# Seven-product block form for three gate pairs and half of the values, and 512-wide values for the rest

## The chip, the cores and the metric

The kernel runs on one core of one Trainium2 chip. The metric is the device time of one execution in microseconds (us). The engines are TensorE (PE in the profile; PEld is its loading of weights), VectorE (DVE), ScalarE (ACT), GpSimd (POOL) and SyncE (SP), which issues most transfers.

## The reference

A trunk of two layers over 512 frames of width 1024. Layer 0 is a gated linear recurrence with 8 heads of 128, layer 1 attends over a shared K and V; each is followed by an MLP (1024 to 4096 and back) with squared ReLU, and every part is normed before and after. The change touches the recurrence's projections alone:

```python
proj = h @ w_in                                   # h: rms_norm(x), 512 x 1024; w_in: 1024 x 4096
q, f, i, g = split(proj, 4)                       # each 512 x 1024, 8 heads of 128 columns
q = silu(q); log_f, k = from f
S_t = diag(f_t) S_(t-1) + k_t v_t^T;  o_t = S_t^T q_t      # v = i, chunk by chunk
o = rms_norm(o, gate_norm_w) * silu(g)
out = o @ w_out
```

## The kernel before

Everything is float32. A product in full precision is made of three matmuls (`mm3`): both operands are split into a high part and a remainder (`whi`, `wlo` for weights, `xhi`, `xlo` for the normed input, `uhi`, `ulo` for what the next projection reads), and high x high, high x remainder and remainder x high are added up in PSUM. x is kept transposed, 128 rows by 8 blocks `kt` by 512 frames. The scale 1/rms of each frame is applied after the projections: `rb` along a row, `rcol` as a column.

Weights come in pieces of 512 KB. `fetch_w` loads a piece into one of four `raw` slots through SyncE's queue; a split writes it into one of eight `whi` and one of eight `wlo` slots. `split_w` does it by a ScalarE copy (high part) and a VectorE subtraction (remainder). `load_d` does it by two ScalarE copies (minus the high part into `wlo`, then the high part) and a transfer issued by POOL that adds the same weights from memory onto `wlo`. A slot is free again when the last matmul that reads it is done.

The order of TensorE's instructions is written out by hand. A `Plan` keeps a clock `t` that each matmul advances by a planned duration; `main` yields work, chains that are spawned (one per head, `head`) come in when their planned time is there, and `until(...)` holds back whoever yields it until keys are `done`. The constants `W_...` are the planned waits. What chains issue on the other engines is put ahead of other work there.

In the recurrence (`hgrn`) `main` goes through four pairs p of heads: the projections `qf` of q and f of both heads (`wmm`, weights stationary, 512 frames moving), then the pair's values `i` (`xmm`, x stationary, 256 columns moving, so that frames become rows), then its gates `g` (weights stationary, 512 wide). A head's chain is: gating of q and f by `gate`; then seven levels of doubling length (`gl`), each some matmuls, two VectorE products and a masked copy (first `g0` with `qc`, at the end a transposition `kt`, and `rec` is done); then, once the pair's gates are there, the state `st`, the output `o`, `head_norm` (`hn_a`) and `store_u` into `uhi`, `ulo`, after which `mix` is done. The head after next starts its levels when `mix` is done. The series of products `tt` of each head runs on POOL.

```python
            if p >= 1:
                yield until(("rec", 2 * p - 1))
            if p >= 2:
                yield until(("mix", 2 * p - 4), ("mix", 2 * p - 3))
            wv = (load_w(w_i[p], 256, None, f"wi{p}") if p == 0 else load_d(w_i[p], 256, f"wi{p}"))
```

After the last gates comes the out-projection `ao_h` (`by_halves`): for the first 256 frames it goes over `kt`, 24 matmuls of 256 columns each, and waits for `mix` of head 6 before step 6 and of head 7 before step 7.

At the start `first_loads` brings in x and the first weights, and `start` makes the sum of squares (`squares`), `rcol`, and from it through `dg` and the matmul `ps_sp` the row `rb`, for which the first two heads wait. PSUM has four banks of tag `mm` (`mmt`) and four of tag `sm` (`smt`). The MLP's up-projection already uses a seven-product block form (class `Pair`, tiles `ux`, `uy`, `uz`): a 2 x 2 block product by seven products of blocks (256 frames by half of the columns by half of the rows) and sums of blocks.

## Time and profile before

| what | value |
| --- | --- |
| median of 3 runs | 1274.45 us (1273.57 to 1278.37) |
| the profiled execution | 1276.38 us, its span 1274.6 us |
| PE busy | 1252.4 us, 98% |
| DVE busy | 786.4 us, 62% |
| ACT busy | 660.9 us, 52% |
| POOL busy | 94.0 us, 7% |
| moved by DMA | 160.37 MB, mean 126 GB/s |

The recurrence takes the first 260 us or so of the span. In a group's row the columns are line, engine, operation, output and inputs, shape and count, then busy time, mean duration in ns of one and the idle time before them with what ended it. A row of waits names who waited for whom, the total, the times and the longest. A row of the chain or of a timeline begins with its start and length in us. In the rows by stretch each engine's busy time stands with its number of instructions, then PE's granted clock, the share of DMA time and GB/s. Durations of matmuls in groups include their pipeline; the rate is read from the chain, as length over count.

### The profile page before, as it was taken

To read this page: it belongs to the slowest core of one execution; us is meant where nothing else is said; L and a number is where in the kernel's file an instruction comes from. 1 tells how busy PE (TensorE), PEld (TensorE's weight loads), DVE (VectorE), ACT (ScalarE), POOL (GpSimd) and SP (SyncE) were. 2 spreads that over 40 slices of the span, in tenths; PEclk is the share of its full clock that TensorE was granted. 3 is DMA by queue.
4 is the path that set the end of the run, shared out by engine and by line. 5 is a ranking of instruction groups with operands and counts; after the bars stand their busy time and mean duration, and the time that the engine had idled before them with its cause. 6 is when DMAs were issued, how large, how long until landed. Compare 5 with 4: busy or idle time off the path is not lost.

```text
span 1274.6 us, 21364 instructions
## 1 busy us (share of the span) xinstructions
PE 1252.4 (98%) x8452; PEld 1135.6 (89%) x8452; DVE 786.4 (62%) x1590; ACT 660.9 (52%) x1222; POOL 94.0 (7%) x169
## 2 busy tenths in 40 slices
PE   9999999999999999999999999999999999999996
PEld 7889898999988989989999788889998998988996
DVE  6866556747954635637388977663875463654645
ACT  6553635237832724616356876663773461561732
POOL 0221212010000000000100000001000000000000
PEclk9999999999999999999999999999999999999998
DMA  7655654224366564635525322232425454463522
GB/s 241 165 129 120 148 129 105 67 76 140 113 166 127 164 142 110 182 83 149 182 76 190 115 85 84 83 98 69 166 100 149 100 179 102 116 182 83 160 89 67
DMA packets 56438, 160.37 MB, mean 126 GB/s; under 512 B 6385, under 2 KB 8690, under 8 KB 56338
## 3 DMA queue, kind: packets, MB, share of 16 engines
q1 hardware_dynamic: 45008, 119.82, 30.2%
q0 software_dynamic: 11088, 39.07, 14.8%
q8 instruction: 66, 1.08, 0.3%
q14 instruction: 34, 0.28, 0.1%
q10 hardware_dynamic: 242, 0.13, 0.0%
HBM read 149.29 MB, written 9.70 MB: 125 GB/s over the span
## 4 chain that ended last, share of the span: by engine, by line
PE 83%; DMA 7%; DVE 4%; ACT 4%; issue 2%; SPq 0%; DVEq 0%; ACTq 0%; POOLq 0%
PE dn L114 20%; PE up L114 7%; PE dn_h L114 7%; PE ux L114 6%; PE kq L114 6%; PE qf L114 5%; PE g L114 4%; DMA raw_s<-in_w_us_dram 4%; PE i L114 3%; PE bo_h L114 3%; PE ao_h L114 3%; PE uz L114 3%; PE gl L114 3%; PE v L114 3%; PE lg L114 2%
## 5 line engine op out<-in xcount | busy, mean ns | idle before, releaser
L114 PE MATMUL dn<-uhi,whi_dn 128*128 128x512 f32 x384 | 151.9, 396 | 0.0
L114 PE MATMUL dn<-uhi,wlo_dn 128*128 128x512 f32 x384 | 151.9, 396 | 0.0
L114 PE MATMUL dn<-ulo,whi_dn 128*128 128x512 f32 x384 | 151.8, 395 | 0.0
L114 PEld LDWEIGHTS dn<-uhi,whi_dn 128*128 128x128 f32 x384 | 72.1, 188 | 17.8 <-ACT r L555 0.7
L482 ACT ACTIVATE whi_a<-raw_a 128x1024 fp32r<-128x1024 f32 x24 | 25.4, 1060 | 120.3 <-PE dn L114 116.6
L114 PEld LDWEIGHTS dn<-uhi,wlo_dn 128*128 128x128 f32 x384 | 72.1, 188 | 17.5
L114 PEld LDWEIGHTS dn<-ulo,whi_dn 128*128 128x128 f32 x384 | 72.1, 188 | 16.9
L170 DVE TENSOR_TENSOR wlo_dn<-raw_dn,whi_dn 128x1024 fp32r<-128x1024 f32 x64 | 76.6, 1220 | 6.3 <-ACT whi_dn L169 4.6
L447 DVE TENSOR_TENSOR ulo<-r,uhi 128x1024 fp32r<-128x1024 f32 (+1 forms) x40 | 40.2, 1010 | 56.7 <-ACT uhi L446 56.7
L114 PE MATMUL up<-xhi,whi_up 128*128 128x256 f32 x256 | 72.7, 284 | 0.0
L114 PE MATMUL up<-xhi,wlo_up 128*128 128x256 f32 x256 | 72.0, 281 | 0.0
L114 PE MATMUL up<-xlo,whi_up 128*128 128x256 f32 x256 | 71.9, 281 | 0.0
L169 ACT ACTIVATE whi_dn<-raw_dn 128x1024 fp32r<-128x1024 f32 x64 | 65.8, 1052 | 7.5 <-PE up L114 3.0
L114 PE MATMUL dn_h<-uhi,whi_dn 128*128 128x256 f32 x240 | 67.8, 282 | 0.0
L114 PE MATMUL dn_h<-ulo,whi_dn 128*128 128x256 f32 x240 | 67.4, 281 | 0.0
L114 PE MATMUL dn_h<-uhi,wlo_dn 128*128 128x256 f32 x240 | 67.4, 281 | 0.0
L602 DVE TENSOR_TENSOR zacc<-dn,zacc 128x512 f32<-128x512 f32 x32 | 22.1, 691 | 59.1 <-PE dn L114 59.0
L504 POOL DMA_DIRECT2D raw_s<-in_w_us_dram x24 | 20.8, 866 | 493.8 <-DMA raw_s<-in_w_us_dram 268.0
L114 PE MATMUL qf<-xhi,whi_qf 128*128 128x512 f32 x128 | 52.9, 413 | 0.8 <-ACT xhi L673 0.6
L482 ACT ACTIVATE whi_t<-raw_a 128x1024 fp32r<-128x1024 f32 x24 | 25.5, 1061 | 49.4 <-PE dn L114 27.2
L114 PE MATMUL qf<-xlo,whi_qf 128*128 128x512 f32 x128 | 50.7, 396 | 0.3 <-DVE xlo L674 0.3
L114 PE MATMUL qf<-xhi,wlo_qf 128*128 128x512 f32 x128 | 50.6, 396 | 0.0
(387 smaller groups left out, 4082.2 us busy)
## 6 DMA issues: line engine op xcount, KB each, us to landing
raw_dn<-in_w_dn_dram SPq DMA_DIRECT2D x64, 512.0 KB, 4.6
raw_a<-in_w_us_dram SPq DMA_DIRECT2D x24, 512.0 KB, 4.4
raw_s<-in_w_us_dram SPq DMA_DIRECT2D x48, 256.0 KB, 4.2
raw_s<-in_w_us_dram POOLq DMA_DIRECT2D x24, 512.0 KB, 6.4
raw_up<-in_w_up_dram SPq DMA_DIRECT2D x16, 512.0 KB, 3.7
raw_wkv<-in_w_kv_dram SPq DMA_DIRECT2D x16, 512.0 KB, 3.8
raw_qf<-in_w_qf_dram SPq DMA_DIRECT2D x14, 512.0 KB, 5.8
raw_d<-in_w_us_dram SPq DMA_DIRECT2D x12, 512.0 KB, 4.2
```

The costliest lines, as they stand in the source:

```text
L114: nc.tensor.matmul(out, lhsT, rhs, **kw)
L169: last_split[:] = [a.activation(hi, raw, AF.Copy)]
L170: v.tensor_tensor(lo, raw, hi.bitcast(F32), op=ALU.subtract)
L447: v.tensor_tensor(ulo[pr][:, :, lo:hi], r, uhi[pr][:, :, lo:hi].bitcast(F32), op=ALU.subtract)
L482: a.activation(hi, raw, AF.Copy)
L504: g.dma_start(rs, ws[p, :, 0:2, :], accum_op=ALU.add)
L602: v.tensor_tensor(z, pss[n4], z, op=ALU.add)
```

## The change

The gates of pairs 1 to 3 (`gates_pair`) and the values of pairs 2 and 3 together (`values_pairs`) are computed by seven block products each, 256 wide, over four blocks of weights and sums of them; the weights lie in memory as four blocks (`w_gs`, `w_is`). Of the sums, those with three or more terms are made by VectorE, and the first ones by a transfer issued by POOL that adds one block onto another in `raw`. Blocks as they are go through `split_d` (as in `load_d`), sums through `split_b` (ScalarE copy, VectorE subtraction). The four sums of x's blocks, with the gains applied, are made once by `block_sums`, a chain that is spawned when the first values are done; they use two `raw` slots while they are made, and three of them stay in `whi` and `wlo` slots, the fourth in `uhi[3]`, `ulo[3]`. x itself stays in the memory of `uhi` (`xraw`) for that, so `squares` no longer overwrites it. The values of pairs 0 and 1 are computed together in pair 0, 512 columns wide. `main` no longer waits for `rec` and `mix` ahead of the values but for `po` (the outputs `o` are issued) and `mix` ahead of the values and gates. `ea`, a row used from the out-projection on, shares the memory of `rb`.

```diff
+    xraw = [cp.tile([P, 2, S], F32, tag=f"uhi{i}", name=f"xraw{i}", bufs=1) for i in range(4)]
+    uhi = [cp.tile([P, 2, S], F32R, tag=f"uhi{i}", name=f"uhi{i}", bufs=1) for i in range(4)]
...
+    nrcol = cp.tile([P, 4], F32, name="nrcol")
+    ea = rb
...
+    def split_d(raw, src, name):
+        n, ncols = raw.shape[1:]
+        hi = wp.tile([P, n, ncols], F32R, tag="whi", name=f"whi_{name}", bufs=8)
+        lo = wp.tile([P, n, ncols], F32R, tag="wlo", name=f"wlo_{name}", bufs=8)
+        a.activation(lo, raw, AF.Copy, scale=-1.0)
+        a.activation(hi, raw, AF.Copy)
+        g.dma_start(lo, src.bitcast(F32R), accum_op=ALU.add)
+        return [(hi[:, j, :], lo[:, j, :]) for j in range(n)]
+    def split_b(raw, name):
+        n, ncols = raw.shape[1:]
+        hi = wp.tile([P, n, ncols], F32R, tag="whi", name=f"whi_{name}", bufs=8)
+        lo = wp.tile([P, n, ncols], F32R, tag="wlo", name=f"wlo_{name}", bufs=8)
+        a.activation(hi, raw, AF.Copy)
+        v.tensor_tensor(lo, raw, hi.bitcast(F32), op=ALU.subtract)
+        return [(hi[:, i, :], lo[:, i, :]) for i in range(n)]
...
-        xs = [hp.tile([P, S], F32, tag="g", name=f"raw_x{kt}", bufs=4) for kt in range(2)]
-        x2 = [wp.tile([P, 2, S], F32, tag="raw", name="raw_x2", bufs=4)]
-        x2 += [hp.tile([P, 2, S], F32, tag="sc", name=f"raw_x{2 * pr}", bufs=2) for pr in (2, 3)]
-        xs += [t[:, j, :] for t in x2 for j in range(2)]
+        xs = [xraw[kt // 2][:, kt % 2, :] for kt in range(8)]
...
-        sq = [hp.tile([P, 2, S], F32, tag="vt", name=f"sqx{pr}", bufs=2) for pr in range(2)]
+        sq = [hp.tile([P, 2, S], F32, tag="vt", name=f"sqx{pr}", bufs=3) for pr in range(4)]
         with tc.issue_after(last_split[0].ins):
-            for kt in range(4):
-                a.activation(sq[kt // 2][:, kt % 2], xs[kt], AF.Square)
-            for kt in range(4, 8):
-                a.activation(xs[kt], xs[kt], AF.Square)
-        v.tensor_tensor(sq[0], sq[0], sq[1], op=ALU.add)
-        for i in range(2):
-            v.tensor_tensor(xs[4 + i], xs[4 + i], xs[6 + i], op=ALU.add)
-            v.tensor_tensor(sq[0][:, i], sq[0][:, i], xs[4 + i], op=ALU.add)
+            for pr in range(4):
+                a.activation(sq[pr], xraw[pr], AF.Square)
+        for pr in range(1, 4):
+            v.tensor_tensor(sq[0], sq[0], sq[pr], op=ALU.add)
...
+    def block_sums(xs, ts):
+        gain = gn[:, G_APRE:G_APRE + 8]
+        e, f = [wp.tile([P, 4, 256], F32, tag="raw", name=f"sum_x{i}", bufs=4) for i in range(2)]
+        def split(src, sign, n):
+            if n < 3:
+                hi, lo = [wp.tile([P, 4, 256], F32R, tag=t, name=f"{t}_x{n}", bufs=8) for t in ("whi", "wlo")]
+            else:
+                hi, lo = [u[3].rearrange("p j (r t) -> p (j r) t", r=2) for u in (uhi, ulo)]
+            a.activation(hi, src, AF.Copy, scale=sign)
+            if sign > 0:
+                v.tensor_tensor(lo, src, hi.bitcast(F32), op=ALU.subtract)
+            else:
+                v.scalar_tensor_tensor(lo, src, -1.0, hi.bitcast(F32), op0=ALU.mult, op1=ALU.subtract)
+            ts.append([(hi[:, r, :], lo[:, r, :]) for r in range(4)])
+        def odd(n, out, op):
+            for r in range(4):
+                v.scalar_tensor_tensor(out[:, r], xs[2 * r + 1][:, n * 256:n * 256 + 256], gain[:, 2 * r + 1:2 * r + 2],
+                                       out[:, r], op0=ALU.mult, op1=op)
+        for r in range(4):
+            for n, t in enumerate((e, f)):
+                a.activation(t[:, r], xs[2 * r][:, n * 256:n * 256 + 256], AF.Copy, scale=gain[:, 2 * r:2 * r + 1])
+        v.tensor_tensor(e, e, f, op=ALU.subtract)
+        split(e, 1.0, 0)
+        yield 8.0
+        odd(1, f, ALU.subtract)
+        split(f, 1.0, 1)
+        yield 8.0
+        odd(1, e, ALU.add)
+        split(e, -1.0, 2)
+        yield 8.0
+        odd(0, e, ALU.subtract)
+        split(e, -1.0, 3)
...
+            done(("po", h))
...
+        def banks(name):
+            return [mmt(f"{name}_{n}") for n in "xyz"]
+        def gates_pair(p):
+            src, nm = w_gs[p - 1], f"gs{p}"
+            ra = wp.tile([P, 2, 512], F32, tag="raw", name=f"raw_a{nm}", bufs=4)
+            nc.sync.dma_start(ra, src[:, 0:3:2, :])
+            rs = wp.tile([P, 2, 512], F32, tag="raw", name=f"raw_s{nm}", bufs=4)
+            for i in range(2):
+                nc.sync.dma_start(rs[:, i, :], src[:, 3, :])
+            g.dma_start(rs, src[:, 0:2, :], accum_op=ALU.add)
+            rd = wp.tile([P, 1, 512], F32, tag="raw", name=f"raw_d{nm}", bufs=4)
+            nc.sync.dma_start(rd, src[:, 1:2, :])
+            a11, a12 = split_d(ra, src[:, 0:3:2, :], f"a{nm}")
+            s3, s1 = split_b(rs, f"s{nm}")
+            v.tensor_tensor(ra[:, 0, :], ra[:, 0, :], rs[:, 1, :], op=ALU.add)
+            v.tensor_tensor(ra[:, 1, :], ra[:, 1, :], ra[:, 0, :], op=ALU.add)
+            s2, s4 = split_b(ra, f"t{nm}")
+            a22, = split_d(rd, src[:, 1:2, :], f"d{nm}")
+            x, y, z = [b[:, 0:256] for b in banks(nm)]
+            g0, g1 = ggs[2 * p], ggs[2 * p + 1] = [hp.tile([P, S], F32, tag="g", name=f"g_{2 * p + j}", bufs=4) for j in range(2)]
+            lo, hi = slice(0, 256), slice(256, 512)
+            t1, t3, t2, t4 = ts
+            def prod(ps, w, b, first):
+                for k in range(4):
+                    mm3(ps, w[0][:, k * P:(k + 1) * P], w[1][:, k * P:(k + 1) * P], *b[k], first and k == 0, k == 3, True)
+                    yield 0
+            def swish(gg, sign):
+                if sign > 0:
+                    v.tensor_tensor(gg, gg, rb, op=ALU.mult)
+                else:
+                    v.scalar_tensor_tensor(gg, gg, -1.0, rb, op0=ALU.mult, op1=ALU.mult)
+                e = hp.tile([P, S], F32, tag="e", name=f"e{nm}{sign}", bufs=1)
+                a.activation(e, gg, AF.Sigmoid)
+                v.tensor_tensor(gg, gg, e, op=ALU.mult)
+            yield from prod(x, a11, xpart(0, 0), True)
+            a.activation(g0[:, lo], x, AF.Copy)
+            yield from prod(z, s1, t1, True)
+            a.activation(g1[:, hi], z, AF.Copy)
+            yield from prod(y, a12, xpart(1, 0), True)
+            v.tensor_tensor(g0[:, lo], y, g0[:, lo], op=ALU.add)
+            yield from prod(x, s2, t2, False)
+            a.activation(g0[:, hi], x, AF.Copy)
+            yield from prod(z, s4, xpart(1, 1), False)
+            v.tensor_tensor(g0[:, hi], z, g0[:, hi], op=ALU.add)
+            swish(g0, 1)
+            yield from prod(x, s3, t3, False)
+            v.tensor_tensor(g1[:, hi], x, g1[:, hi], op=ALU.add)
+            a.activation(g1[:, lo], x, AF.Copy)
+            yield from prod(y, a22, t4, True)
+            v.tensor_tensor(g1[:, lo], y, g1[:, lo], op=ALU.add)
+            swish(g1, -1)
+        def values_pairs():
+            nm = "is"
+            def raw(n):
+                return wp.tile([P, 1, 1024], F32, tag="raw", name=f"raw_{n}{nm}", bufs=4)
+            def block(n, i):
+                r = raw(n)
+                nc.sync.dma_start(r, w_is[:, i:i + 1, :])
+                return r
+            def summed(n, i):
+                r = block(n, 3)
+                g.dma_start(r, w_is[:, i:i + 1, :], accum_op=ALU.add)
+                return r
+            ra = block("a", 0)
+            a11, = split_d(ra, w_is[:, 0:1, :], f"a11{nm}")
+            rs = summed("s1", 1)
+            s1, = split_b(rs, f"s1{nm}")
+            rb_ = block("b", 2)
+            a12, = split_d(rb_, w_is[:, 2:3, :], f"a12{nm}")
+            v.tensor_tensor(ra, ra, rs, op=ALU.add)
+            s2, = split_b(ra, f"s2{nm}")
+            v.tensor_tensor(rb_, rb_, ra, op=ALU.add)
+            s4, = split_b(rb_, f"s4{nm}")
+            s3, = split_b(summed("s3", 0), f"s3{nm}")
+            a22, = split_d(block("d", 1), w_is[:, 1:2, :], f"a22{nm}")
+            x, y, z = [b.rearrange("p (m f) -> p m f", m=2) for b in banks(nm)]
+            v0, v1 = vts[2], vts[3] = [hp.tile([P, 4, 256], F32, tag="vt", name=f"vt{p}", bufs=3) for p in (2, 3)]
+            t1, t3, t2, t4 = ts
+            def prod(ps, w, b, first):
+                for m in range(2):
+                    for k in range(4):
+                        f = slice(k * 256, k * 256 + 256)
+                        mm3(ps[:, m, :], *[t[:, m * P:(m + 1) * P] for t in b[k]], w[0][:, f], w[1][:, f],
+                            first and m == 0 and k == 0, k == 3, True)
+                        yield 0
+            def keep(out, ps, n, r):
+                for m in range(2):
+                    tt = 2 * n + m
+                    a.activation(out[:, tt, :], ps[:, m, :], AF.Copy, scale=r[:, tt:tt + 1])
+            def more(out, ps, n, r):
+                for m in range(2):
+                    tt = 2 * n + m
+                    v.scalar_tensor_tensor(out[:, tt, :], ps[:, m, :], r[:, tt:tt + 1], out[:, tt, :], op0=ALU.mult, op1=ALU.add)
+            yield from prod(x, a11, xpart(0, 0), True)
+            keep(v0, x, 0, rcol)
+            yield from prod(z, s1, t1, True)
+            keep(v1, z, 1, nrcol)
+            yield from prod(y, a12, xpart(1, 0), True)
+            more(v0, y, 0, rcol)
+            yield from prod(x, s2, t2, False)
+            keep(v0, x, 1, rcol)
+            yield from prod(z, s4, xpart(1, 1), False)
+            more(v0, z, 1, rcol)
+            yield from prod(x, s3, t3, False)
+            more(v1, x, 1, nrcol)
+            keep(v1, x, 0, nrcol)
+            yield from prod(y, a22, t4, True)
+            more(v1, y, 0, nrcol)
...
-            if p >= 1:
-                yield until(("rec", 2 * p - 1))
-            if p >= 2:
-                yield until(("mix", 2 * p - 4), ("mix", 2 * p - 3))
-            wv = (load_w(w_i[p], 256, None, f"wi{p}") if p == 0 else load_d(w_i[p], 256, f"wi{p}"))
-            vt = vts[p] = hp.tile([P, 4, 256], F32, tag="vt", name=f"vt{p}", bufs=2)
-            for t2 in range(2):
-
-                ps = (smt if p == 0 else mmt)(f"i{p}_{t2}").rearrange("p (j t) -> p j t", j=2)
-                yield from values(ps, wv, t2)
-                if p == 0 and t2 == 0:
-                    yield until("rcol")
-                keep_values(vt, ps, t2)
             if p == 0:
+                wv = load_w(w_i, 512, None, "wi")
+                vts[0], vts[1] = [hp.tile([P, 4, 256], F32, tag="vt", name=f"vt{i}", bufs=3) for i in range(2)]
+                for tt in range(4):
+                    ps = (smt if tt < 2 else mmt)(f"i{tt}")
+                    for kt in range(8):
+                        xmm(ps, wv, kt, 512, tt * P, kt == 0, kt == 7)
+                        yield 0
+                    if tt == 0:
+                        yield until("rcol")
+                    for i in range(2):
+                        a.activation(vts[i][:, tt, :], ps[:, i * 256:(i + 1) * 256], AF.Copy, scale=rcol[:, tt:tt + 1])
                 yield until("rb")
-            wt = load_d(w_g[p], 256, f"wg{p}") if p else load_w(w_g[p], 256, None, f"wg{p}")
-            for j in range(2):
-                ps = mmt(f"g{p}_{j}")
-                for kt in range(8):
-                    wmm(ps, wt, kt, j * P, xhi, xlo, 0, S, kt == 0, kt == 7)
-                    yield 0
-                gg, sg = gate(ps, "g", 2 * p + j)
-                v.tensor_tensor(gg, gg, sg, op=ALU.mult)
-                ggs[2 * p + j] = gg
+                spawn(block_sums(xs, ts), 2.0)
+                wt = load_w(w_g, 256, None, "wg")
+                for j in range(2):
+                    ps = mmt(f"g0_{j}")
+                    for kt in range(8):
+                        wmm(ps, wt, kt, j * P, xhi, xlo, 0, S, kt == 0, kt == 7)
+                        yield 0
+                    gg, sg = gate(ps, "g", j)
+                    v.tensor_tensor(gg, gg, sg, op=ALU.mult)
+                    ggs[j] = gg
+            else:
+                yield until(("po", 2 * p - 2), ("po", 2 * p - 1))
+                if p >= 2:
+                    yield until(("mix", 2 * p - 4), ("mix", 2 * p - 3))
+                if p == 2:
+                    yield from values_pairs()
+                yield from gates_pair(p)
```

The argument lists, the layout of the weights on the host and the moved helper `xpart` are left out here.

More of the change, by code (lines that the diff above doesn't have):

```diff
@@ L186, in load_d, with xpart @@
         for pr in range(ncols // 128):
-            raw = fetch_w(src, ncols, pr, name)
-            hi = wp.tile([P, per, ncols], F32R, tag="whi", name=f"whi_{name}_{pr}", bufs=8)
-            lo = wp.tile([P, per, ncols], F32R, tag="wlo", name=f"wlo_{name}_{pr}", bufs=8)
-            a.activation(lo, raw, AF.Copy, scale=-1.0)
-            a.activation(hi, raw, AF.Copy)
-            g.dma_start(lo, src[:, per * pr:per * (pr + 1), :].bitcast(F32R), accum_op=ALU.add)
-            out += [(hi[:, j, :], lo[:, j, :]) for j in range(per)]
-        return out
+            out += split_d(fetch_w(src, ncols, pr, name), src[:, per * pr:per * (pr + 1), :], f"{name}_{pr}")
+        return out
+    def xpart(j, n):
+        lo, hi = halves[n]
+        return [(xhi[r][:, j, lo:hi], xlo[r][:, j, lo:hi]) for r in range(4)]
     def load_w(src, ncols, gain, name):
@@ L451, in block @@
         b11, b12, b21, b22 = [zb[:, :, j, lo:hi] for j in range(2) for lo, hi in halves]
-        def xpart(j, n):
-            lo, hi = halves[n]
-            return [(xhi[r][:, j, lo:hi], xlo[r][:, j, lo:hi]) for r in range(4)]
         def sums_x():
@@ L475, in sums_x @@
             return parts
-        def split_b(raw, name):
-            n = raw.shape[1]
-            hi = wp.tile([P, 2, 512], F32R, tag="whi", name=f"whi_{name}", bufs=8)[:, 0:n, :]
-            lo = wp.tile([P, 2, 512], F32R, tag="wlo", name=f"wlo_{name}", bufs=8)[:, 0:n, :]
-            a.activation(hi, raw, AF.Copy)
-            v.tensor_tensor(lo, raw, hi.bitcast(F32), op=ALU.subtract)
-            return [(hi[:, i, :], lo[:, i, :]) for i in range(n)]
         a22s = []
@@ L709, in start @@
         rsqrt_col(mean_cols([ssum[:, j, :] for j in range(2)], S, onesd), EPS, rcol)
+        v.tensor_scalar(nrcol, rcol, -1.0, None, op0=ALU.mult)
         done("rcol")
@@ L1064, in main @@
             spawn(start(hp, xs, maskf))
-            yield from hgrn(hp, w0)
+            yield from hgrn(hp, w0, xs)
             proj = out_proj(w_ao, gn[:, G_GATE:G_GATE + 1], "ao",
```

24 lines of the change are left out of this document (13 added, 11 removed).

## The prediction

> **What bounds the kernel now.** I read four views in this order: the head of the page, the engines' waits up to 300 us, the chain that ended last in order of time, and the timelines of single engines where the chain leaves TensorE.
>
> ```profile
> span 1274.6 us, 21364 instructions
> PE 1252.4 (98%) x8452; PEld 1135.6 (89%) x8452; DVE 786.4 (62%) x1590; ACT 660.9 (52%) x1222; POOL 94.0 (7%) x169
> PE ps_sp L114 <- DVE dg L713: 1.2, 1, 1.2
> ...
> 98.00:160.00 62.00, 62.00 (x405) 55.13 (x404) 35.31 (x95) 29.45 (x58) 10.15 (x20) 1.00 0.60 135
> ```
>
> TensorE is busy 98% of the span at full clock. After its 1.2 us wait for `dg` (at about 35 us, the longest that the list has up to 300 us) it does not stop in the recurrence: in 98 to 160 it is busy 62.00 of 62.00 us, with VectorE at 35.31 and ScalarE at 29.45. So what the change takes off TensorE counts in full, and every stall that it makes counts in full too. The chain gives the rates:
>
> ```profile
> 36.82 9.11 PE i L114 x78
> 204.52 11.19 PE qf L114 x48
> 404.60 1.43 PE ux L114 x12
> 406.02 1.44 PE uz L114 x12
> ```
>
> (start, length, instructions.) A 512-wide matmul takes 11.19/48 = 0.2331 us, a 256-wide one of the values 9.11/78 = 0.1168, and one of the seven-product form (already used in the MLP) 1.435/12 = 0.1196. Width costs in proportion, the last form 2.5% more.
>
> **The change part by part.**
>
> Matmuls. A gate pair was 2 x 8 x 3 = 48 at 0.2331 = 11.19 us; it becomes 7 x 4 x 3 = 84 at 0.1196 = 10.05. Three pairs: -3.4 us. Values of the last four heads: 192 become 7 x 2 x 4 x 3 = 168, same form as `i` (x stationary): 24 x 0.1168 = -2.8. Values of the first four: 192 at 0.1168 = 22.43 become 96 of 512 at 0.2331 = 22.38: -0.05. Together **-6.3 us**. The page on matmuls would have it otherwise:
>
> By the Trainium skill ("TensorE: Matmul & The Clock Gate", "Back-to-back issue gap") a sustained stream spaces N=128 at about 81 ns and N=512 at about 131, so a straight line gives about 98 for 256, an estimate. A gate pair would then go from 6.3 to 8.2 us and be a loss, and the term would be +5.8 - 2.3 - 6.2 = -2.7. The rows above (233 ns and 117 to 120) do not agree, and I take the rows.
>
> The start. Here the trace shows how tight the recurrence's first chain is (VectorE's timeline, then ScalarE's, then VectorE by stretches):
>
> ```profile
> 27.45 0.16 DVE L225 TENSOR_SCALAR nx<-ps_mc 128x4 f32<-128x4 f32 x1 [2.30 <-PE ps_mc L114]
> 27.53 1.23 DVE L170 TENSOR_TENSOR wlo_wi<-raw_wi,whi_wi 128x1024 fp32r<-128x1024 f32 x1
> ...
> 33.82 1.23 DVE L170 TENSOR_TENSOR wlo_qf<-raw_qf,whi_qf 128x1024 fp32r<-128x1024 f32 x1 [0.18 <-ACT whi_qf L169]
> 34.96 0.68 DVE L713 TENSOR_TENSOR dg<-ident,rcol 128x512 f32<-128x512 f32 x1
> 47.08 0.43 ACT L772 ACTIVATE qc<-q 128x256 f32<-128x256 f32 x1
> 47.87 2.76 PE L114 MATMUL g<-qc,k 128*128 128x192 f32 x16
> ...
> 20.00:30.00 10.00, 10.00 (x53) 8.42 (x52) 7.36 (x12) 7.08 (x9) 0.00 (x0) 1.00 0.55 188
> 30.00:40.00 10.00, 8.81 (x60) 7.68 (x59) 8.25 (x17) 4.47 (x5) 0.00 (x0) 1.00 0.81 268
> 40.00:50.00 10.00, 10.00 (x74) 9.59 (x74) 8.88 (x16) 9.20 (x16) 6.90 (x16) 1.00 0.43 144
> ```
>
> From 27.45 `rcol`'s eleven small operations run one after the other up to `dg` at 34.96, and five weight splits of about 1.23 us (the first and the last stand here) have slipped in between. TensorE waits for `dg`, and the last `qc` (ready 47.51) is used at 47.87, a margin of 0.4. The change puts two more splits of `w_i` before this, and `block_sums`: on VectorE one subtraction (1.23 by L170's form), twelve of 128x256 (0.42, as L808 below) and four splits (1.23) = 11.2 us; on ScalarE eight scaled copies (0.47, as `vt` below) and four splits of 1.05 (L190's form, below) = 8.0.
>
> ```profile
> L808 DVE TENSOR_TENSOR k<-k,tt 128x256 f32<-128x256 f32 x48 | 20.2, 420 | 0.0
> L911 ACT ACTIVATE vt<-i,rcol 128x256 f32<-128x256 f32 x16 | 6.6, 467 | 16.6 <-PE i L114 16.6
> ```
>
> VectorE has 30 - 7.36 - 8.25 - 8.88 = 5.5 us free between 20 and 50. `block_sums` waits for no data but x, so part of it lands in the gaps of the two chains, and part in 50 to 80, where the levels have room. Least: 0 (all of it later; below nothing is excluded, as it only adds work there). Most: each of the six gaps that are still unfilled takes one more split of 1.05 net, 6.3. The nearest row is the wait of before, 1.2 us with five of eleven gaps filled; with two or so more filled I take **+2.0**. The squares cost the same, since four 128x1024 activations replace eight halves; `nrcol` is one operation of 0.16 beside them.
>
> Evictions. Each product is copied or added out by an operation of 0.42 to 0.47 us; a bank is read again two or three products later (1.43 us each), except `x` between the second block of sums and the next product, with one product between. A split of 1.05 us ahead of it on ScalarE makes 1.05 + 0.47 = 1.52, 0.1 late, three times. The rest of ScalarE's and VectorE's new work per stage (some 4 us each) lies beside TensorE (62.00 against 35.31). `ea` in `rb`'s place and x in `uhi`'s cost nothing: no instruction is added, `uhi`'s next writer is the first head's store behind its whole chain, and `ea` is first written after the out-projection.
>
> Weights' ring. x's sums pin three of the eight `whi`/`wlo` slots until the last gate pair, so five go round. Two of the four raw slots serve the sums at the start only.
>
> ```profile
> L190 ACT ACTIVATE wlo_qf<-raw_qf x8: 1041/1044/1051, 84.1 to 163.1; 128x1024 fp32r<-128x1024 f32 x8
> L192 POOL DMA_DIRECT2D wlo_qf<-in_w_qf_dram x8: 862/870/880, 85.5 to 164.5; - x8
> DMA to landing us min/median/max: 7.4/8.0/9.6
> ...
> 85.48 0.88 POOL L192 DMA_DIRECT2D wlo_qf<-in_w_qf_dram x1 [4.29 <-ACT os_a L626]
> 133.36 2.80 PE qf L114 x12
> ```
>
> From a free slot to a usable block: two copies of 1.05, 0.87 to issue, 8.0 to land = 11.0 us. Before, the block issued at 85.48 is read at 133.36, 40 us after landing. After, a value block lasts 24 x 0.1168 = 2.8 us, four blocks ahead are 11.2, and the heads' own matmuls stretch that. Of 62 us the main stream has 4 x 11.2 = 44.8, so the factor is 62/44.8 = 1.38 and the lead 15.5 us against 11.0. I take **+0.3** with the evictions; ends 0 and, late by 1 us on each of the eleven accumulated blocks of the last two stages, +11. SyncE issues four loads per gate pair instead of two and five for the values instead of four, each waiting for a raw slot as before. POOL issues three accumulating transfers per gate pair instead of two and five for the values instead of four (0.87 each); the new one into `raw_s` waits for the loads under it, and behind it stand the `tt` products of the next head:
>
> ```profile
> 145.97 0.61 POOL L811 TENSOR_TENSOR tt<-ek 128x256 f32<-128x256 f32 x1 [9.64 <-DVE nt L231]
> 158.98 1.30 PE g L114 x8
> ```
>
> They run 13 us before that head's first matmul, so a landing of 8 us in front of them is covered, and I count nothing.
>
> The tail. The last two heads lose 11.2 us of values as cover.
>
> ```profile
> 225.56 0.35 PE i L114 x3
> 231.87 0.65 PE g L114 x4
> ...
> 258.01 0.33 PE kt L119 x3
> 261.88 1.34 PE st L114 x12
> 263.56 3.12 PE o L114 x28
> 279.56 0.44 PE hn_a L119 x4
> 272.05 0.37 ACT L626 ACTIVATE os_a<-o,yh 128x128 f32<-128x128 f32 x1 [0.42 <-DVE os_a L624]
> 281.91 0.69 DVE L636 TENSOR_TENSOR ulo<-g,uhi 128x512 fp32r<-128x512 f32 x1 [0.70 <-ACT uhi L635]
> ```
>
> From the end of the last `qf` (225.56) head 7 needs 6.3 to its first matmul (231.87), 26.5 to the end of its levels (258.34), 3.5 to `st`, 4.8 to the end of `o` (266.68), 5.7 to its normed rows (272.42; the order holds `hn` back until 279.56, but they are ready), 0.44, and 2.6 to `ulo` (282.60): 49.8 us. TensorE has in that time: gates 10.05, out-projection steps 0 to 6, 7 x 24 x 0.1168 = 19.6, and two heads at 8.6 (half of 62 - 44.8 = 17.2) = 46.9. So it idles 49.8 - 46.9 = 2.9 before the last step; before, with 11.2 more values and 1.1 more gates, cover was 59. Ends: 0 (if the levels come nearer to the 23.0 us of head 6) and +8 (if `hn` is held for the planned time). **+2.9.**
>
> Sum: -6.3 + 2.0 + 0.3 + 2.9 = -1.1. The profiled execution took 1276.38 us (span 1274.6), so 1275.3; it lay 1.9 above the median of the three runs, 1274.45, from which -1.1 gives **1273.3**.
>
> **The rivals.** *Nothing is given back*: start and tail hide in what the scheduler finds. For it: TensorE shows no wait from 37 to 290 now, and the order by hand leaves head 7 12.9 us from `o` to `hn` (266.68 to 279.56) where 5.7 suffice. Against: margin 0.4 at `qc`, and 2.9 short at the tail. 1274.45 - 6.3 = 1268.1. *The ring starves* (slower): accumulated blocks come late in the stages with values and last gates. For it: a lead cut from 40 us to 15.5; ScalarE already sits waiting for slots (7.9 us in the row below), with the chain's activations queued behind. Against: 15.5 is over 11.0. It decides when queues on ScalarE and POOL add more than 4.5 us; eleven blocks late by 1 us each: 1273.3 + 11 = 1284.3.
>
> ```profile
> ACT wlo_wi L190 <- PE i L114: 7.9, 3, 7.3
> ```
>
> *Half-width products cost more than half*: the page's rule, as a term of -2.7 instead of -6.3: 1273.3 + 3.6 = 1276.9. The MLP's rows speak against it. That the change does not do what it says I exclude but for the values' first half, which is no saving.
>
> **How the numbers follow.** A measurement of this kernel tells about 0.5% (6.4 us) from no change. Forecast 0.57, nothing given back 0.20, ring 0.20, half-width 0.03. Faster needs under 1268.1: most of the second case, 0.17. Slower needs over 1280.8: most of the ring and a little of the forecast's upper end, 0.23. Else 0.60. The range: below, -6.3 with half a us for what else may shift, 1267.5; above, start 6.3, tail 4 and ring 4 against -6.3 are +8, 1282.5, which leaves out the ring's worse half. The forecast's own range is 1269 to 1278.
>
> **What would show it.** Right: gate products at 1.43 us per 12, 10.0 us per pair; a wait for `dg` of 2 to 4 us near 36; a gap of 1 to 4 us before the out-projection's last step, released by `ulo`; that step's end about 4 us earlier than 287.5. Wrong: TensorE waiting for `whi` or `wlo` in the stages of heads 4 to 7 (ring), waits at `gl` for VectorE (sums in the levels), or no waits at all (then 1268).

## The result, and the profile after

The changed kernel takes 1282.2 us (median of 5 runs, 1281.38 to 1283.12) against 1273.94 us of the kernel before on the same chip: a ratio of 1.0059, interval 1.0041 to 1.0076. The forecast was 1273.3 and "no change"; the time lies in its range, at the upper end, but it moved the other way: 8.3 us slower where 1.1 us faster was forecast. The profiled execution took 1281.38 us.

The head of the page after, TensorE's three longest waits in the recurrence, and its busy time in the stretch up to the first matmul of `up` (busy time with instructions, granted clock, DMA share, GB/s):

```profile
span 1279.3 us, 21468 instructions
PE 1241.0 (97%) x8440; PEld 1125.2 (88%) x8440; DVE 820.6 (64%) x1646; ACT 674.1 (53%) x1248; POOL 100.2 (8%) x171
PE o L114 <- DVE st L879: 11.5, 3, 6.3
PE g L114 <- ACT qc L812: 1.8, 2, 1.3
PE qf L114 <- DMA wlo_qf<-in_w_qf_dram: 1.4, 1, 1.4
0.00:326.50 326.50, 307.55 (x2040) 0.97 0.48 127
```

TensorE is busy 11.4 us less than before (1241.0 against 1252.4) and the span is 4.7 us longer. Up to the first matmul of `up` it is busy hardly less (307.55 us against 307.88), so most of the 11.4 lies behind the recurrence, and in the recurrence waits came. The wait for `dg` is no longer in the list; in its place stands one of 11.5 us, `o` for `st`, in three pieces. Where they lie is read from TensorE's timeline, and what held `st` from VectorE's, POOL's and SyncE's:

```profile
217.69 0.39 PE L114 MATMUL o<-vt,sc 128*128 128x128 f32 x2
224.41 0.80 PE L114 MATMUL o<-st,q 128*128 128x128 f32 x2 [6.33 <-DVE st L879]
...
213.13 0.69 DVE L936 TENSOR_TENSOR g<-g,egs2-1_2039 128x512 f32<-128x512 f32 x1 [0.93 <-ACT egs2-1_2039 L935]
223.41 0.69 DVE L915 TENSOR_TENSOR raw_ags<-raw_ags,raw_sgs 128x512 f32<-128x512 f32 x1 [9.58 <-DMA raw_sgs<-in_w_gs_dram]
224.01 1.12 DVE L879 SCALAR_TENSOR_TENSOR st<-st,tt,st 128x128 f32<-128x128 f32 x4
...
207.12 0.81 SPq L909 DMA_DIRECT2D raw_sgs<-in_w_gs_dram  x2
216.07 0.85 POOL L910 DMA_DIRECT2D raw_sgs<-in_w_gs_dram  x1 [5.02 <-DMA raw_sgs<-in_w_gs_dram]
```

`st` itself is 1.12 us of work and its inputs are there. But in VectorE's queue the addition of L915 stands ahead of it, and that waits for `raw_sgs`: the two loads under it are issued at 207.12, POOL can issue the accumulating transfer at 216.07, and it lands at 223.4. For 9.58 us VectorE does nothing, with `st` of two heads behind the addition, and TensorE stands 6.33 us. At 87 to 92.5 the same picture costs 4.84 us:

```profile
90.33 0.69 DVE L915 TENSOR_TENSOR raw_ags<-raw_ags,raw_sgs 128x512 f32<-128x512 f32 x1 [7.63 <-DMA raw_sgs<-in_w_gs_dram]
92.54 0.80 PE L114 MATMUL o<-st,q 128*128 128x128 f32 x2 [4.84 <-DVE st L879]
```

The waits cost more than their length. Rows by stretch (busy time of PE, PEld, DVE, ACT, POOL, then PE's granted clock):

```profile
92.00:98.00 6.00, 5.46 (x28) 5.14 (x29) 3.19 (x19) 2.28 (x16) 0.00 (x0) 0.72 0.03 6
...
219.00:224.00 5.00, 0.00 (x0) 0.00 (x0) 0.59 (x1) 0.00 (x0) 0.00 (x0) 0.50 1.07 216
224.00:228.00 4.00, 3.59 (x17) 3.59 (x18) 2.36 (x10) 1.14 (x8) 0.00 (x0) 0.50 0.87 162
228.00:232.00 4.00, 4.00 (x19) 3.40 (x19) 2.77 (x17) 1.55 (x10) 0.00 (x0) 0.91 0.00 0
...
300.00:304.00 4.00, 4.00 (x24) 4.00 (x23) 0.69 (x1) 2.79 (x6) 0.00 (x0) 0.57 0.01 4
300.00:326.50 26.50, 26.50 (x218) 26.40 (x217) 17.41 (x33) 18.87 (x38) 2.19 (x4) 0.94 0.18 62
```

After the second wait the clock is 0.50 for four more microseconds. Time lost by the clock is length times what it lacks: behind these two waits 6 x 0.28 + 4 x 0.50 + 4 x 0.09 = 4.0 us. The last two rows belong to another wait, that of the out-projection ahead of 299.55 (shown further down): 26.5 x 0.06 = 1.6 us, nearly all of it in the first four microseconds.

The Trainium skill ("TensorE: Matmul & The Clock Gate", "Part 1: The HAM clock gate") has it that an idle window of some 3.4 us brings the clock to half. The trace agrees on the half, 0.50, and shows that it can come without so long a wait ahead of it: the row from 219 on has 0.50 already, 0.9 us after TensorE's last matmul ended (217.69 + 0.39; the 1.4 us of waiting for `wlo_qf` lie shortly before it), and the out-projection's wait was 1.8 us.

The first matmul of `up` comes at 326.5 instead of 311.2, 15.3 us late. Yet the kernel ends only 4.7 us late. The reason stands in the chain. Before and after, the first line is the tile's row (count: least, median and greatest duration in ns, first and last start), the second a stage of the MLP that the change does not touch, from the chain (start, length, instructions):

```profile
L114 PE MATMUL up<-xhi,whi_up x256: 277/281/468, 311.2 to 957.3; 128*128 128x256 f32 x128
615.87 27.68 PE dn_h L114 x234
```

```profile
L114 PE MATMUL up<-xhi,whi_up x256: 275/281/471, 326.5 to 968.4; 128*128 128x256 f32 x128
630.79 26.52 PE dn_h L114 x234
```

The same 234 matmuls take 118.3 ns each before and 113.3 ns after, at full clock. So two things that the prediction did not have work against each other: a queue and a speed-up of untouched matmuls.

### The profile page after: what moved, and what is told of

It is laid out like the page before. It is cut to its first block, busy times and chain, and to the rows that moved or that the text cites. A ratio compares the mean times of both kernels' runs of the same rounds, so it can differ in the third digit from the quotient of the medians.

```text
span 1279.3 us, 21468 instructions
## 1 busy us (share of the span) xinstructions
PE 1241.0 (97%) x8440; PEld 1125.2 (88%) x8440; DVE 820.6 (64%) x1646; ACT 674.1 (53%) x1248; POOL 100.2 (8%) x171
## 4 chain that ended last, share of the span: by engine, by line
PE 64%; DVE 5%; ACT 4%; DMA 3%; issue 2%; DVEq 0%; ACTq 0%; POOLq 0%; SPq 0%
PE dn L114 21%; PE ux L114 7%; PE up L114 7%; PE kq L114 6%; PE dn_h L114 5%; PE bo_h L114 3%; PE uz L114 3%; PE ao_h L114 3%; DMA raw_s<-in_w_us_dram 3%; PE v L114 2%; PE lg L114 2%; PE uy L114 1%; PE ao L114 1%; DVE wlo_s L200 1%; PE pt L119 1%
## 5 line engine op out<-in xcount | busy, mean ns | idle before, releaser
L114 PEld LDWEIGHTS dn<-ulo,whi_dn 128*128 128x128 f32 x384 | 72.3, 188 | 16.8
```

The costliest lines, as they stand in the source:

```text
L114: nc.tensor.matmul(out, lhsT, rhs, **kw)
```

## The experiments

**The queue.** The theory: the addition ahead of `st` costs 11.5 us of waits and 3 to 4 us of clock. The rival: the waits are of the ring (slots and transfers), and another place in the queue only moves them.

*e1: the additions issued behind `st`.*

```diff
+                last_st[:] = [v.scalar_tensor_tensor(st[:, c, :], ...)]
...
+            with tc.issue_after(last_st[0].ins):
+                v.tensor_tensor(ra[:, 0, :], ra[:, 0, :], rs[:, 1, :], op=ALU.add)
```

(and so for the other additions onto `ra` and `rb_`)

> The additions onto raw_a (pairs of gates, and values) are put behind the last two state operations st in VectorE's queue; nothing else is changed. Theory Q (queue): TensorE's 11.5 us of waits of o for st are st standing behind an addition that waits for a transfer into raw_s, and the granted clock of 0.50 to 0.72 after the two long ones is their consequence. Then these waits go, the clock stays near 1.00, and the time falls by 11.5 + 3 to 4, from 1282 to about 1267. Rival L (late ring): the transfers are simply too late because the ring is short; the wait then moves to the gate products (gs waiting for wlo_s or wlo_t) or to the head norm behind the additions, and the time stays above 1277.

Measured 1265.37 us, ratio 0.993 (0.9915 to 0.9945), 16.8 below the changed kernel. VectorE's timeline, and TensorE by stretch where the wait was:

```profile
86.56 1.47 DVE L879 SCALAR_TENSOR_TENSOR st<-st,tt,st 128x128 f32<-128x128 f32 x4 [0.76 <-ACT st L877]
90.55 0.69 DVE L917 TENSOR_TENSOR raw_ags<-raw_ags,raw_sgs 128x512 f32<-128x512 f32 x1 [2.53 <-DMA raw_sgs<-in_w_gs_dram]
...
92.00:98.00 6.00, 6.00 (x27) 4.83 (x26) 5.41 (x28) 2.80 (x6) 1.02 (x2) 1.00 0.03 6
```

The transfer lands as late as before (90.5) and hurts nobody, since `st` has gone ahead; the clock is 1.00 and `up` begins at 310.1. The queue is shown.

*e3: x's block sums off the weights' ring* (in the memory of `ulo[0]`, `ulo[1]`; additions left ahead of `st`).

```diff
+    sumx = [cp.tile([P, 4, 256], F32, tag=f"ulo{i}", name=f"sum_x{i}", bufs=1) for i in range(2)]
...
-        e, f = [wp.tile([P, 4, 256], F32, tag="raw", name=f"sum_x{i}", bufs=4) for i in range(2)]
+        e, f = sumx
```

> The two working tiles of x's block sums lie in the memory of ulo[0] and ulo[1] instead of two of the four raw slots; all else as changed. Theory Q with raw slots as the cause of the first late transfer: the loads into raw_s of the first gate pair go out some 8 us earlier (about 69 instead of 77 us), the first wait of o for st (6 us near 86) is gone with its slow clock (1.7 us), the third one near 219 stays: about 1274. Rival L: the weights' ring of eight with three pinned is what delays, and both waits stay: 1280 to 1282.

Measured 1280.33 us, ratio 1.0046 (1.0031 to 1.0062): missed. The waits of `o` fell only to 8.4 us, and the start paid for it:

```profile
PE o L114 <- DVE st L880: 8.4, 3, 7.9
PE ps_sp L114 <- DVE dg L754: 3.0, 1, 3.0
PE qf L114 <- DVE xlo L680: 1.9, 2, 1.6
```

So the slots that the sums hold made the first transfer late, but not the others; and with a place at once the sums fill VectorE ahead of `dg`, as e4 shows below.

*e4: both edits.*

> Both edits, additions behind st and sums off the raw slots. Theory Q: as the first edit alone, since without the order no late transfer reaches TensorE: about 1267, within 2 us of it. Rival L: the raw slots matter by themselves, and it is faster than the first alone by 4 us or more.

Measured 1271.36 us, ratio 0.9976 (0.9966 to 0.9987): also missed, by the same 3.0 us at `dg` and the waits around it. VectorE reaches `dg` six microseconds later than in e1 (the first two lines are of e4, the third of e1):

```profile
15.13 1.22 DVE L721 TENSOR_TENSOR sum_x<-sum_x,sum_x 128x1024 f32<-128x1024 f32 x1
39.45 0.69 DVE L754 TENSOR_TENSOR dg<-ident,rcol 128x512 f32<-128x512 f32 x1
33.51 0.68 DVE L753 TENSOR_TENSOR dg<-ident,rcol 128x512 f32<-128x512 f32 x1
```

That the sums queue for `raw` slots is what keeps them off the first chain.

**The untouched matmuls.** `ea` in the place of `rb` takes 2048 bytes out of each partition and `nrcol` adds 32, so that all later tiles move. Theory: the new addresses make the matmuls faster. Rival: something in the block products does.

*e2: the kernel before in the layout of after.*

```diff
-    ea = cp.tile([P, S], F32, name="ea")
+    nrcol = cp.tile([P, 4], F32, name="nrcol")
+    ea = rb
```

> The kernel before with one thing of the change alone: the row ea lies in rb's memory, and a column nrcol is allocated, so that everything behind them in SBUF lies some 2 KB lower; no instruction of the computation changes. Theory A (addresses): the 256-wide matmuls outside the recurrence, which went from 119.4 ns to 115 to 117 ns in the changed kernel, did so because of where the tiles lie; then they do so here too, and the time falls by some 8 to 10 us, to about 1264. Rival N (not the addresses but what happened before, or the order of the other engines): the spacing stays at 119 ns and the time within 2 us of the kernel before.

Measured 1266.7 us, ratio 0.9941 (0.9926 to 0.9956). No instruction differs but one `memset`; 7.5 us go by addresses alone. e5 and e6 part the two shifts.

*e5: 32 bytes alone. e6: `ea` in `rb` alone.*

```diff
+    pad = cp.tile([P, 4], F32, name="pad")      # e5
...
-    ea = cp.tile([P, S], F32, name="ea")
+    ea = rb      # e6
```

> The kernel before with nothing changed but an unused tile of 16 bytes a partition (32 with its padding) ahead of ea, so that every tile of the pools behind it starts 32 bytes later: the weights' parts whi and wlo start at 105920 of a partition (a multiple of 64) where they started at 105888 (32 more than a multiple of 64). Theory alignment (what sped up the 256-wide matmuls in the layout of after is that those parts begin on a multiple of 64 bytes): 1266.7 us within 2, the spacing of dn_h<-uhi,whi_dn's matmuls 112.5 ns for 117.5, their median duration 276 ns for 280. Rival, the shift by 2 KB (where tiles lie to each other or in larger blocks): no change, 1274 within 2, spacing 117.5.

> The kernel before with ea laid into rb's place and no new tile: every tile behind moves 2048 bytes down, and whi and wlo start at 103840, still 32 more than a multiple of 64. Theory alignment: 1274 us within 2, dn_h's spacing 117.5 ns. Rival, the shift by 2 KB: 1266.7 within 2, spacing 112.5.

e5 measured 1265.49 us, ratio 0.9941 (0.9926 to 0.9956); e6 1273.33 us, ratio 1.0001 (0.9992 to 1.001). One unused tile of 16 bytes makes the kernel 0.6% faster. The tile's rows of e5 and e6 (least, median, greatest duration in ns):

```profile
L114 PE MATMUL dn_h<-uhi,whi_dn x240: 276/276/468, 612.3 to 1248.6; 128*128 128x256 f32 x120
```

```profile
L114 PE MATMUL dn_h<-uhi,whi_dn x240: 277/280/466, 615.7 to 1255.9; 128*128 128x256 f32 x120
```

*e11: e8 (e1 with the sums of x later, below) with `whi` and `wlo` on a multiple of 128. e10: e5 with only the ring's tiles at their new place, those of the pools behind it 32 off again.*

```diff
-    nrcol = cp.tile([P, 4], F32, name="nrcol")
+    nrcol = cp.tile([P, 20], F32, name="nrcol")[:, 0:4]
```

```diff
+    pd = ctx.enter_context(tc.tile_pool(name="pd", bufs=1))
+    pad2 = pd.tile([P, 8], F32, name="pad2")
```

> e8_sums_of_x_later with 64 bytes of padding more: whi and wlo start at 103936, a multiple of 128, for 103872, a multiple of 64 alone. Theory, that 64 bytes are what counts: 1263.3 us within 1.5, the same. Rival, that 128 bytes would be better still: 1260 or less.

> e5_pad_32_bytes with another 32 bytes between the pool of the weights and the pools that follow it: raw, whi and wlo begin on a multiple of 64, every tile of the recurrence, the MLP and the attention is again 32 off. Theory, that only the operand that TensorE loads (the weights' parts) counts: 1265.5 us within 1.5, spacing of dn_h<-uhi,whi_dn 112.5 ns. Rival, that the moving operands or the other engines' tiles count (t, kq, at, zacc): between 1267 and 1273.

e10: 1266.23 us, ratio 0.995 (0.9934 to 0.9966), as expected: the ring's place is enough. e11: 1272.65 us, ratio 0.9991 (0.9981 to 1.0): the theory of 64-byte alignment fell, as a multiple of 128 is as slow as 32 off. In all fast kernels so far `whi` lay at 64 past a multiple of 128 and `uhi` on one (bytes within a partition). The table below has the distance of `whi`, which TensorE loads, from `uhi`, which moves through it.

*Three more on top of e8. e13: everything moved by 64. e15: `whi`, `wlo` and what follows moved by 32 more. e14: only the pools behind the ring moved by 64.*

```diff
+    pad0 = cp.tile([P, 16], F32, name="pad0")      # e13: ahead of xhi
...
+    nrcol = cp.tile([P, 12], F32, name="nrcol")[:, 0:4]      # e15
...
+    pad2 = pd.tile([P, 16], F32, name="pad2")      # e14: between the ring and the pools behind it
```

> e8_sums_of_x_later with 64 unused bytes ahead of xhi: every tile moves by 64, so xhi, xlo, uhi, ulo start at 64 past a multiple of 128 and whi, wlo on a multiple of 128. Theory relative (what counts is the place of the loaded operand against that of the moving one, modulo 128 bytes: 64 apart is fast): all distances are those of e8, 1263.3 us within 1.5, spacing of dn_h<-uhi,whi_dn 112.7 ns. Theory absolute (whi and wlo must start at an odd multiple of 64): as e11_parts_on_128, 1272.6 within 2, 118 ns.

> e8_sums_of_x_later with 32 bytes more ahead of whi and wlo, which start at 96 past a multiple of 128, 96 from u and x (the tiles that follow move too, so t stays 0 from the parts). Theory relative, the fourth distance: in e10_parts_alone_aligned t lay 32 above the parts (they 96 from it) and ux<-t,whi_s took 116.6 ns, so dn_h about 116 and the time between e8 and e11, 1267 within 3. Theory absolute: any place other than 64 past a multiple of 128 is slow, 1272.6 within 2.

> e8_sums_of_x_later with 64 unused bytes between the pool of the weights and the pools that follow: u, x and whi, wlo stay (64 apart), the tiles of the recurrence, the MLP and the attention move from 64 past a multiple of 128 to 0, so the MLP's sums t, which are moving operands with whi_s and whi_t loaded, lie 64 from these for 0 before. Theory relative: the spacing of ux<-t,whi_s, ux<-t,whi_t and uz<-t,whi_s falls from 118.4 ns to 113 to 115, some 2600 matmuls of them by 3.5 to 5 ns = 9 to 13 us at most, 1253 us within 4. Theory absolute (the parts' own place counts): 1263.3 within 1.5.

| kernel | `uhi` mod 128 | `whi` mod 128 | distance | median of dn_h's matmul, ns | us |
| --- | --- | --- | --- | --- | --- |
| e11 | 0 | 0 | 0 | 281 | 1272.65 |
| before | 0 | 32 | 32 | 280 | 1273.94 |
| e5 | 0 | 64 | 64 | 276 | 1265.49 |
| e13 | 64 | 0 | 64 | 276 | 1264.91 |
| e15 | 0 | 96 | 96 | 280 | 1274.57 |
| e14 | 0 | 64 | 64 | 281 | 1265.94 |

The rows of e11, e13 and e15:

```profile
L114 PE MATMUL dn_h<-uhi,whi_dn x240: 279/281/470, 616.2 to 1256.1; 128*128 128x256 f32 x120
```

```profile
L114 PE MATMUL dn_h<-uhi,whi_dn x240: 276/276/468, 611.0 to 1245.2; 128*128 128x256 f32 x120
```

```profile
L114 PE MATMUL dn_h<-uhi,whi_dn x240: 277/280/469, 617.8 to 1257.9; 128*128 128x256 f32 x120
```

(before and e5 are without the block products.) e13, with a ratio of 0.9932 (0.9913 to 0.9951), tells the distance from the place: `whi` on a multiple of 128 is slow with `uhi` on one (e11) and fast with `uhi` 64 past one. Of four distances only 64 was ever fast; e15 (ratio 1.0009, 1.0 to 1.0018) shows that it is not graded.

e14 was to use the same for the MLP's sums `t`, and missed: 1265.94 us, ratio 0.9951 (0.9934 to 0.9969), where 1253 was hoped for. The rows of `t` as the moving operand, of e14 and of e8:

```profile
L117 PE MATMUL uz<-t,whi_s x192: 279/280/284, 402.8 to 1195.7; 128*128 128x256 f32 x192
```

```profile
L114 PE MATMUL uz<-t,whi_s x192: 274/282/287, 405.9 to 1197.7; 128*128 128x256 f32 x192
```

The median went from 282 to 280 ns only. The trace has 864 matmuls with `t` moving (three groups of 192 and three of 96) where some 2600 were expected, so even the whole of 3.5 to 5 ns would have given 3 to 4 us and not 9 to 13. And e14 has an exception in `dn_h` itself: `uhi` and `whi` lie 64 apart as in e8, and the median is 281. The row, then TensorE in 22 us of `dn_h` in the first MLP and in the second (busy time of PE, PEld, DVE), and a like stretch of the first MLP in e8:

```profile
L117 PE MATMUL dn_h<-uhi,whi_dn x240: 276/281/468, 610.6 to 1245.6; 128*128 128x256 f32 x120
612.00:634.00 22.00, 22.00 (x189) 22.00 (x188) 2.11 (x4) 1.00 0.39 128
1205.00:1227.00 22.00, 22.00 (x197) 22.00 (x196) 2.05 (x3) 1.00 0.13 46
```

```profile
614.00:636.00 22.00, 22.00 (x197) 22.00 (x196) 2.06 (x4) 1.00 0.42 138
```

In e14 the first MLP's `dn_h` is slow (189 matmuls in 22 us) and the second's fast (197), with the same distance and the full clock in both. So a distance of 64 bytes does not make it fast by itself; something else counts too, and no run here shows what. With x as the moving operand it is mixed: `uz<-xhi,whi_t` gains (the rows of before and of e5), `up<-xhi,whi_up` keeps its median of 281 (the rows of before and after, above).

```profile
L114 PE MATMUL uz<-xhi,whi_t x96: 278/283/285, 410.2 to 1214.3; 128*128 128x256 f32 x96
```

```profile
L114 PE MATMUL uz<-xhi,whi_t x96: 276/276/286, 409.5 to 1206.0; 128*128 128x256 f32 x96
```

What is shown is that moving the ring by some bytes against x and u is worth 7.5 us and more; a rule by which the speed of each product could be foretold is not shown, and why 64 bytes matter is open.

**What the change is worth without both.** *e7: e1 with `nrcol` in the padding behind `rcol`, so that the ring lies 32 off as before. e9: the changed kernel in that layout.*

```diff
-    rcol = cp.tile([P, 4], F32, name="rcol")
-    nrcol = cp.tile([P, 4], F32, name="nrcol")
+    rcol2 = cp.tile([P, 2, 4], F32, name="rcol")
+    rcol, nrcol = rcol2[:, 0, :], rcol2[:, 1, :]
```

> The changed kernel with the two additions of block sums issued behind st (as in e1_adds_after_st) and nrcol laid into the padding behind rcol, so that whi and wlo start at 103840, 32 more than a multiple of 64, as they did before. What is left of the change is the block products, the sums of x and their ring without the wait in VectorE's queue and without the new place in memory. Theory (alignment and queue add up): the time of before less 1.1 to 1.3 us, 1273 within 2, up starting at 310.1 within 1. Rival, that the block products gain from the new places themselves, or that the gain of 8.8 us of e1_adds_after_st has a third part: below 1270, or above 1276.

> The changed kernel with its additions where they stood (ahead of st in VectorE's queue), and nrcol laid into the padding behind rcol, so that whi and wlo start at 103840, 32 more than a multiple of 64 bytes, as they did before: the change without the gift of its 16 new bytes. Theory (queue and alignment add up): after's 1282.2 plus the 7.5 to 8 us that the alignment was worth in e2 and e5 = 1290 us within 2, ratio to before 1.013, the wait o<-st 11 us in three. Rival, that alignment is worth less where the queue stalls: 1285 or less.

e7: 1273.35 us, ratio 1.0004 (0.9994 to 1.0014). e9: 1290.15 us, ratio 1.0132 (1.0113 to 1.015). The corners add up (e5 and e1 from above; the kernel before measured 1273.06 to 1274.18 beside the various runs, 1273.08 beside e5 and e7):

| | ring 32 off | ring 64 from u and x |
| --- | --- | --- |
| before | 1273.08 | 1265.49 (e5) |
| change, additions behind `st` | 1273.35 (e7) | 1265.37 (e1) |
| change as made | 1290.15 (e9) | 1282.2 |

Down the columns the queue costs 16.8 us in both; across the rows the addresses give 7.6 to 8.0; the block products alone cost 0.3 or give 0.1, nothing that can be measured.

*e8: e1 with the sums of x later. e12: e8 with the values of the last four heads 512 wide.*

```diff
-        yield 8.0
+        yield 18.0
```

```diff
-                    yield from values_pairs()
+                    wv = load_d(w_i[1], 512, "wj")
+                    ... 4 x 8 steps xmm(ps, wv, kt, 512, tt * P, kt == 0, kt == 7) into vts[2], vts[3]
```

> e1_adds_after_st with one number changed: the generator of x's block sums rests 18 instead of 8 of its planner's units after its first sum, so that the multiply-adds and conversions of sums two to four stand behind the operations of qc of heads 0 and 1 on VectorE and ScalarE. Theory (the wait g<-qc of 1.8 us comes of those operations ahead of qc): the wait goes, 1.5 us faster than e1_adds_after_st, 1264 within 1.5. Rival: the sums hold two slots of the raw ring 10 us longer, the loads of qf's weights for heads 2 and 3 come later, a wait of qf for wlo_qf of 2 us or more takes its place, 1265.4 or slower.

> e8_sums_of_x_later with the values of the last four heads not by block products but 512 wide like those of the first four (96 matmuls of 128x512, 22.4 us by 0.2333 each, for 168 of 128x256, 19.6 by 0.1168): no accumulating transfers for them, no additions, seven evictions less. By the prediction's term (values -2.8, given back by the tail's missing cover 2.8 to 2.9): 1263.3 us within 1.5, the same. Rival, that the values' saving is kept: 1266. Rival, that their sums and additions cost more than they save: 1261 or less.

e8: 1263.25 us, ratio 0.9927 (0.9912 to 0.9942), the fastest kernel here, ahead of both. `g` waits 0.5 us for `qc` instead of 1.8, but `up` begins at 310.8, 0.7 later than in e1, so the 2.1 us are not shown to come from that wait; the runs of e1 and e8 overlap. In the profiled execution of e8 the clock fell behind the out-projection's wait, in that of e1 it did not: the same 65 matmuls take 9.27 and 7.66 us.

```profile
283.84 9.27 PE ao_h L114 x65
```

```profile
284.74 7.66 PE ao_h L114 x65
```

e12: 1267.21 us, ratio 0.9962 (0.9951 to 0.9972), missed: without the block form of the values it is 4.0 us slower by the medians and 1.5 by the profiled spans (1264.4 against 1262.9). Their saving in matmuls was put at 2.8, so at least a good part of it is kept; how much is not settled.

## Why the prediction was wrong, step by step

**The failed step** is in the part on the weights' ring: of the new accumulating transfer into `raw_s` it says that behind it stand the `tt` products, "and I count nothing". That looked at POOL's queue, where the transfer is issued, and not at VectorE's, where the addition that needs its landing is issued by `main` and stands ahead of the chain's `st`. It cost 16.8 us (e1 against the change, e7 against e9): 11.5 of waits, 4.0 of slower clock, and 1.3 that are not told apart. The rival of the starving ring had late blocks and a price of +11, but at the wrong place: it looked for TensorE waiting for `whi` or `wlo`, and only 1.4 us of that came. And no stall was priced with the slower clock behind it, here a third as much again (4.0 us on 11.5).

**"`ea` in `rb`'s place ... cost nothing"** was right by e6 (1273.33). But `nrcol`, priced as one operation of 0.16 us, moved every later tile by 32 bytes, and that was worth -8. Without it the time would have been 1290, beyond the range: the forecast came as near as it did by luck, through two misses of opposite sign.

**The sum itself** was right in what it counted. With the queue mended and the layout kept (e7) it forecasts -1.1, and +0.3 was measured. Its terms are read from TensorE's busy time up to `up`, for the kernel before, e7, e5 and e1:

```profile
0.00:311.20 311.20, 307.88 (x2052) 1.00 0.49 129
```

```profile
0.00:311.80 311.80, 304.47 (x2040) 0.99 0.49 134
```

```profile
0.00:310.80 310.80, 306.39 (x2052) 1.00 0.48 129
```

```profile
0.00:310.10 310.10, 301.76 (x2040) 1.00 0.50 134
```

- Matmuls: -6.3 forecast; -3.4 (before to e7) and -4.6 (e5 to e1) measured. The rate was right (the chain of e1 below: 1.42 us for 12 against 1.43), so width costs in proportion, and the rule of the Trainium skill that the prediction weighed ("TensorE: Matmul & The Clock Gate", "Back-to-back issue gap") does not agree with these rows either; of the missing 2 to 3 us some 1.5 in e7 are the half clock behind the out-projection's wait (65 matmuls of `ao_h` take 9.47 us in e7, 7.96 in e9, which has the same addresses), and what the rest is, is not shown.
- What is given back: +5.2 forecast; idle time up to `up` grew from 3.3 to 7.3 us (before to e7) and from 4.4 to 8.3 (e5 to e1).
- The start: +2.0 forecast as a wait for `dg`. That wait, 1.2 before, went, since the sums wait for `raw` slots (e4 shows 3.0 us where they do not), and 1.8 us of `g` for `qc` came, the place with the margin of 0.4: +0.6.
- The tail: +2.9 forecast; in after TensorE stands from 297.39 to 299.55 but for one matmul, 1.8 us, for head 7's last chain, as described. The half clock that can follow (1.6 us in after, none in e1) was not in the sum.

```profile
237.86 1.42 PE gs_z L114 x12
```

```profile
296.94 0.45 PE hn_a L119 x4
...
298.80 0.70 DVE ulo L643
299.51 0.04 issue
299.55 9.26 PE ao_h L114 x65
```

(the first from the chain of e1, the others from that of after; start, length, work.)

## What to carry to other kernels

When a step is added that waits for a transfer, look at the queue of every engine that consumes its landing, not only of the one that issues it: an addition of 0.69 us that waits 9.6 in an in-order queue holds whatever was written behind it, and issuing it after the urgent work cost nothing and gave 16.8 us. Before an edit is credited or blamed, repeat the kernel before with the addresses that the edit leaves behind: here 16 bytes of an unused column were worth more than the seven-product form. And price a stall of TensorE with the clock behind it.

## What the hardware showed that was not expected

- Where the loaded and the moving operand start, modulo 128 bytes, changes the spacing of 256-wide matmuls in full precision: dn_h's are 113.3 ns apart with the two 64 bytes from each other and 118.3 at 32 (26.52 and 27.68 us for 234), and slow at 0 and 96 as well; from 32 to 64 this was worth 7.5 to 8.0 us of this kernel. It is not the whole rule: in e14 one `dn_h` stage is slow at 64 (189 matmuls in 22 us, 197 in the other stage), and for `t` as the moving operand hardly any gain came (282 to 280 ns).
- After 6.33 us of idleness the granted clock was 0.50, for four microseconds of work more, and 0.91 in the four after that. A wait of 11.5 us in three pieces, with some 4.0 of slower clock behind it and 1.6 behind the out-projection's wait, delayed `up` by 16.4 (326.5 against 310.1 in e1, which was spared all three).
- The same wait of 1.8 us ahead of `ao_h` was followed by a slower clock in the profiled executions of after (0.57 over four microseconds) and e8 (9.27 us for 65 matmuls) and not in that of e1 (7.66).
